# Two-block network on one core: conditioning steps moved from the second feed-forward into the first, and attention values computed token-major

## The chip, the core and the metric

The program runs on one core of a Trainium2 chip. Five engines work side by side, each on its own instructions in program order: PE (TensorE, the matrix engine), DVE (VectorE), ACT (ScalarE), POOL (GpSimd) and SP (SyncE, which here issues nearly all DMA transfers on its queue). They wait for one another by semaphores. The metric is the device time of one execution in microseconds, the median of several runs.

## What is computed

512 tokens of width 1024 go through two blocks in fp32. The first block is feed-forward, mixer, feed-forward. The second is two layers of mixer and mixture of experts, each modulated by vectors made from a condition vector. The two parts that the change touches:

```python
def swiglu(h, w_in, w_out):                      # both feed-forwards of the first block
    g, u = jnp.split(h @ w_in, 2, axis=-1)
    return (jax.nn.silu(g) * u) @ w_out

def adaln(cond, mod_w, mod_b):                   # second block, layer i: mod_w[i] is 1024 x 6144
    m = jax.nn.silu(cond) @ mod_w + mod_b
    return jnp.split(m, 6, axis=-1)
...
sh1, sc1, g1, sh2, sc2, g2 = adaln(c, mod_w[i], mod_b[i])
csh1, csc1, ... = adaln(c_ctx, mod_w[i], mod_b[i])          # layer 0 only, two of six are used
...
def gqa_attend(q, k, v):                         # 8 query heads, 2 key/value heads of width 64
    s = jnp.einsum('bqkgd,bskd->bkgqs', q, k) * (HEAD_DIM ** -0.5)
    p = jax.nn.softmax(s, axis=-1)               # 512 queries against 256 + 512 keys
    return jnp.einsum('bkgqs,bskd->bqkgd', p, v)
...
y = jnp.concatenate([o, multiscale_pool(p, pool_w, pool_scale)], axis=-1) @ w_out
```

## The kernel before

Activations are kept feature-major: a tile has 128 features as partitions and the 512 tokens along the free axis. fp32 products that go through `mm3` (lines 164 to 166) are made from a high and a low part of each operand, three matmuls a step; `hilo` makes the parts, the high one as a cast on ACT (line 159), the low one as a subtraction on DVE (line 160). Weights are loaded by `wload` in tiles of 512 KB into buffers `raw` (line 149, on SP's queue), and `hilo` makes `w` from them.

A feed-forward (`ffn`, line 334) works through the hidden width in four parts of 7, 6, 6 and 3 tiles. In a part, for each tile `gate_up` makes gate and up products (48 matmuls of 512 columns, into a PSUM tile `pb`), `gate` makes the activation tile `act` from them (ACT: silu and cast, DVE: product and low half), and then the down projection runs over eight output tiles, adding to `y` (line 438). The last part is done for one half of the tokens and then the other (h0 and h1, 256 columns); behind each half the boundary normalises: square sums on DVE (line 288), one matmul with ones, a reciprocal square root (lines 261 to 264), the residual (lines 310 and 312) and the input of the next layer (line 299). The mixer that follows starts with h0.

Work that has no place of its own stands in a queue of closures, `bgq`. `ffn` takes `bg` of them behind each tile of `gate_up`, `bg // 3` ahead of each output tile of a down projection, and all that are left ahead of its last part. The modulation vectors are such work: `mv_group` (line 223) queues eight steps for one vector of 1024 entries, each step being one load of 512 KB of `mod_w` into a buffer `aux` (line 231, on SP's queue) and one DVE operation that multiplies it with the silu of the condition (repeated over the partitions, tile `s2`) and sums along the free axis (line 235, 128x1024). For the first two vectors of layer 0 a second such operation does the same with the context's condition (`s3`); its product goes into a buffer `junk` of the pool `k4`, which the tiles `act` come from too. In the kernel before, all 96 steps (112 operations) are queued for the second feed-forward with `bg=5`; the first has `bg=4` and, of the queue, only small preparations of the mixer (`pre_mixer1`).

The attention of the second block (`gqa_head`, line 985) is called for eight heads, four chunks `c` for each of two key/value heads `i`; three streams (the four heads of either `i`, and pooling) are interleaved by `weave`, by written costs. For one head and each of four blocks `n` of 128 queries: the scores go into a PSUM tile `pb` (one of two, 128 queries x 768 keys), DVE takes the maximum (line 998), ACT the exponential with its sum (line 1000) into a buffer `aux` or `raw`, DVE the reciprocal of the sum (line 1001), and DVE or ACT scales the tile by it (lines 1005, 1003). `flip` transposes six blocks on PE (line 1013) and copies them out (lines 1016, 1017). For each two blocks `values` makes six matmuls in plain fp32 (line 1025; each leaves two records in the trace) with the values as weights and 256 query columns moving, into a PSUM tile `pa` of three; ACT copies 64 of its 128 rows to the output tile (line 1026).

The order of the instructions on each engine is set by a scheduler from the order of the code and priorities; it is fixed when the kernel is built.

## Time and profile before

| | us |
|---|---|
| median of 3 runs (1978.03 to 1979.84) | 1978.21 |
| profiled execution, its own time | 1981.37 |
| span of its trace | 1979.5 |
| PE busy | 1829.2 (92%) |
| DVE busy | 1310.9 (66%) |
| ACT busy | 910.8 (46%) |
| mean granted clock of PE | 0.970 of 2.4 GHz |

The stages in that trace, in us from its start: first feed-forward to 402.5, mixer to about 697, second feed-forward to about 1040, mixer of the second block to 1290 (its attention 1135 to 1259), experts to 1550, second layer to the end. With PE busy for 92% of the span, what matters is where it is not, and which other engine or transfer it stands for there. Durations below are those of single instructions; neighbours on an engine overlap by a little, so a stretch of equal ones is best read from start to start.

### The profile page before, as it was taken

To read this page: it belongs to the slowest core of one execution; us is meant where nothing else is said; L and a number is where in the kernel's file an instruction comes from. 1 tells how busy PE (TensorE), PEld (TensorE's weight loads), DVE (VectorE), ACT (ScalarE), POOL (GpSimd) and SP (SyncE) were. 2 spreads that over 40 slices of the span, in tenths; PEclk is the share of its full clock that TensorE was granted. 3 is DMA by queue.
4 is the path that set the end of the run, shared out by engine and by line. 5 is a ranking of instruction groups with operands and counts; after the bars stand their busy time and mean duration, and the time that the engine had idled before them with its cause. 6 is when DMAs were issued, how large, how long until landed. Compare 5 with 4: busy or idle time off the path is not lost. (4 is left out here: it accounts for less than half of the span.)

```text
span 1979.5 us, 25341 instructions
## 1 busy us (share of the span) xinstructions
PE 1829.2 (92%) x9461; PEld 1497.1 (76%) x9461; DVE 1310.9 (66%) x2253; ACT 910.8 (46%) x1463; POOL 163.9 (8%) x133
## 2 busy tenths in 40 slices
PE   4999999999977999989999989979999699979996
PEld 3778888986756888768898867867666688976663
DVE  8877444686775788888448678656654655557773
ACT  5423223465666642222337565526665622345551
POOL 0000000000000000000000000004442000014431
PEclk9999999999998999999999989989999899979998
DMA  8887333232113257888534000538997513559993
GB/s 323 307 311 267 115 93 112 88 120 75 64 32 117 75 191 270 313 315 299 191 106 144 1 0 1 192 131 271 304 319 260 195 60 122 177 202 357 344 353 82
DMA packets 109472, 361.27 MB, mean 183 GB/s; under 512 B 19592, under 2 KB 20256, under 8 KB 109344
## 3 DMA queue, kind: packets, MB, share of 16 engines
q1 hardware_dynamic: 92640, 328.09, 47.0%
q0 software_dynamic: 16128, 29.41, 5.6%
q10 hardware_dynamic: 576, 2.10, 0.3%
q8 instruction: 77, 1.26, 0.3%
q14 instruction: 51, 0.42, 0.1%
HBM read 354.25 MB, written 34.62 MB: 196 GB/s over the span
## 5 line engine op out<-in xcount | busy, mean ns | idle before, releaser
L160 DVE TENSOR_TENSOR w<-raw,w 128x1024 fp32r<-128x1024 f32 (+3 forms) x192 | 221.8, 1160 | 172.5 <-issue 73.1
L159 ACT CAST w<-raw 128x1024 fp32r<-128x1024 f32 (+3 forms) x192 | 191.2, 1000 | 305.4 <-PE pa L166 95.7
L164 PE MATMUL pb<-hh,w 128*128 128x512 f32 (+1 forms) x800 | 288.5, 362 | 19.3 <-ACT hh L159 14.2
L165 PE MATMUL pb<-hl,w 128*128 128x512 f32 (+1 forms) x800 | 289.7, 362 | 4.8 <-DVE hl L160 4.6
L166 PE MATMUL pb<-hh,w 128*128 128x512 f32 (+1 forms) x800 | 289.7, 362 | 2.3 <-DVE w L160 2.3
L164 PEld LDWEIGHTS pb<-hh,w 128*128 128x128 f32 x800 | 151.4, 190 | 45.8 <-ACT hh L159 16.0
L165 PEld LDWEIGHTS pb<-hl,w 128*128 128x128 f32 x800 | 151.7, 190 | 29.7 <-DVE hl L160 7.0
L166 PEld LDWEIGHTS pb<-hh,w 128*128 128x128 f32 x800 | 151.7, 190 | 27.2 <-DVE w L160 4.5
L160 DVE TENSOR_TENSOR k<-raw,k 128x1024 fp32r<-128x1024 f32 x101 | 121.6, 1218 | 65.6 <-ACT k L159 49.1
L164 PE MATMUL pa<-hh,w 128*128 128x512 f32 (+1 forms) x392 | 142.2, 366 | 3.3 <-ACT sq L286 2.0
L1462 PE MATMUL pb<-w,a 128*128 128x512 f32 x304 | 136.9, 593 | 1.9 <-ACT a L1451 1.9
L165 PE MATMUL pa<-hl,w 128*128 128x512 f32 (+1 forms) x392 | 135.5, 347 | 0.0
L166 PE MATMUL pa<-hh,w 128*128 128x512 f32 (+1 forms) x392 | 134.8, 345 | 0.0
L164 PE MATMUL pa<-k,w 128*128 128x512 f32 x304 | 126.3, 415 | 0.0
L235 DVE SCALAR_TENSOR_TENSOR aux<-aux,s 128x1024 f32<-128x1024 f32 x96 | 115.3, 1220 | 16.1 <-DMA aux<-in_mod_w 15.8
L165 PE MATMUL pa<-act,w 128*128 128x512 f32 x304 | 119.1, 392 | 1.8 <-DVE act L160 1.8
L164 PE MATMUL pa<-act,w 128*128 128x512 f32 x304 | 119.1, 392 | 1.6 <-ACT w L159 1.6
L166 PE MATMUL pa<-k,w 128*128 128x512 f32 x304 | 119.8, 394 | 0.0
L166 PE MATMUL pa<-act,w 128*128 128x512 f32 x304 | 119.3, 392 | 0.5 <-DVE w L160 0.5
L165 PE MATMUL pa<-k,w 128*128 128x512 f32 x304 | 119.3, 392 | 0.0
L159 ACT CAST k<-raw 128x1024 fp32r<-128x1024 f32 x101 | 105.2, 1048 | 9.6 <-DMA raw<-in_moe_w 3.3
L1462 PEld LDWEIGHTS pb<-w,a 128*128 128x128 f32 x304 | 57.2, 189 | 60.2 <-issue 53.2
(446 smaller groups left out, 3989.3 us busy)
## 6 DMA issues: line engine op xcount, KB each, us to landing
aux<-in_mod_w SPq DMA_DIRECT2D x96, 512.0 KB
raw<-in_ffn_in SPq DMA_DIRECT2D x88, 512.0 KB
raw<-in_moe_w SPq DMA_DIRECT2D x86, 512.0 KB
aux<-in_w_ada SPq DMA_DIRECT2D x64, 512.0 KB
w<-in_moe_w SPq DMA_DIRECT2D x64, 512.0 KB
k<-in_moe_w SPq DMA_DIRECT2D x42, 512.0 KB
raw<-in_ffn_out SPq DMA_DIRECT2D x32, 384.0 KB
raw<-in_mix_in SPq DMA_DIRECT2D x20, 512.0 KB
```

The costliest lines, as they stand in the source:

```text
L159: self.nc.scalar.copy(hi, src)
L160: return self.nc.vector.tensor_sub(lo, src, hi.bitcast(F32)).ins
L164: mm(p, wh, xh, start=start, stop=False)
L165: mm(p, wh, xl, start=False, stop=False)
L166: mm(p, wl, xh, start=False, stop=stop)
L235: self.nc.vector.scalar_tensor_tensor(junk, w, 1.0, s, op0=OP.mult, op1=OP.mult, accum_out=dst[:, m:m + 1])
L1462: nc.tensor.matmul(py[:, ns], a[:, cs], wt[c][:, ns], start=c == 0, stop=c == 1)
```

## The change

Three vectors of layer 0 (groups 0 to 2 of 12, a quarter) are queued for the first feed-forward, behind `pre_mixer1`: 24 steps with 40 DVE operations, the two silus, and the small sums that end them. The condition tiles come to be known only when their load runs, so `outs` names them and `cvec` holds them. The other 72 steps (72 operations) stay in the second feed-forward, where `s2` is loaded and silu'd again, and `bg` falls from 5 to 3.

In the attention the exponentials are no longer scaled. `values` takes the transposed exponentials as weights (128 keys x 128 queries) and 64 columns of values moving, so that its output has the queries as partitions: for a pair of heads (both `i` of one `c`) eight blocks of 64 columns in one PSUM tile `pt`, the only one of its pool. Behind the pair one reciprocal of the eight columns of sums, one DVE product that scales all 512 columns and moves them to SBUF, four transposes and one ACT copy make the output tile. A pair's values begin when the pair before has both heads done. `flip` now writes one tile `pt` for each block of queries.

```diff
@@ mv_group
                 for i, (s, dst) in enumerate(outs):
+                    s = self.cvec[s] if isinstance(s, str) else s
                     last = i == len(outs) - 1
@@ even mixer
+        pairs = [{"n": 0} for _ in range(4)]
...
-                yield from self.gqa_head(qs[c], i, k, (la, lb)[i], vf, outs[c])
+                pairs[c]["before"] = pairs[c - 1] if c else None
+                yield from self.gqa_head(qs[c], i, k, (la, lb)[i], vf, pairs[c], outs[c])
@@ gqa_head
+        if "l" not in both:
+            both["l"] = self.sm(8, tag="l8", bufs=2)
...
-            nc.scalar.activation(pe[:, :768], sc[:, :768], AF.Exp, bias=mx, accum_out=l)
-            nc.vector.reciprocal(l, l)
-            if (n + 2 * i) % 4 == 0:
-                nc.scalar.activation(pe[:, :768], pe[:, :768], AF.Copy, scale=l)
-            else:
-                nc.vector.tensor_scalar(pe[:, :768], pe[:, :768], l, None, op0=OP.mult)
+            nc.scalar.activation(pe[:, :768], sc[:, :768], AF.Exp, bias=mx, accum_out=both["l"][:, 2 * n + i:2 * n + i + 1])
...
-            t, tx = wt[-1]
+            t = self.k4(F32, "pt")
...
-            a(v3(t, 4)[:, :, js], v3(pt, 4))
-            b(v3(tx, 2)[:, :, js], v3(pc[:, :256], 2))
-        def values(half):
-            t, tx = wt[-1]
-            po = self.psa()[:, :256]
+            a(t[:, :512], pt)
+            b(t[:, 512:768], pc[:, :256])
+            return t
+        def values(n, t):
+            if "po" not in both:
+                assert both["before"] is None or both["before"]["n"] == 2
+                both["po"] = self.pst()
+            o = (2 * n + i) * 64
             for b in range(6):
-                vs = slice(b * P, (b + 1) * P)
-                m = t[:, b * 256:(b + 1) * 256] if b < 4 else tx[:, (b - 4) * 256:(b - 3) * 256]
-                nc.tensor.matmul(po, vf[:, vs], m, start=b == 0, stop=b == 5)
-            nc.scalar.copy(out[r, half * 256:half * 256 + 256], po[r, :])
+                nc.tensor.matmul(both["po"][:, o:o + 64], t[:, b * P:(b + 1) * P], vf[:, b * P + 64 * i:b * P + 64 * i + 64],
+                                 start=b == 0, stop=b == 5)
...
+        l, tk = both["l"], self.pg()
+        nc.vector.reciprocal(l, l)
+        nc.vector.tensor_tensor(tk.rearrange("p (n e) -> p n e", n=8), both["po"].rearrange("p (n e) -> p n e", n=8),
+                                l.unsqueeze(2).to_broadcast((P, 8, 64)), OP.mult)
+        pt = self.psa()
+        for n in range(4):
+            ns = slice(n * P, (n + 1) * P)
+            nc.tensor.transpose(pt[:, ns], tk[:, ns], self.mat("ident"))
+        nc.scalar.copy(out, pt)
@@ main
+        def silus(*which):
+            def go():
+                for n, i in which:
+                    cvec[n] = K.k4(F32, n)
+                    nc.sync.dma_start(cvec[n], A["c_rep"][i])
+                with tc.issue_after(K.gated):
+                    for n, _ in which:
+                        nc.scalar.activation(cvec[n], cvec[n], AF.Silu)
+            return go
...
+        def mod_group(l, g):
+            outs = [("s2", mod[l][g])]
+            if l == 0 and g < 2:
+                outs = [("s3", cmod[g])] + outs
+            K.mv_group(A["mod_w"][l], g, outs)
...
+        K.queue(silus(("s2", 1), ("s3", 2)))
+        for g in range(3):
+            mod_group(0, g)
         K.ffn(h, *ffw("ffn1"), post_boundary(0, to if stop != "ffn1" else None), bg=4, lead=lead)
...
+        K.queue(silus(("s2", 1)))
         for l in range(2):
             for g in range(6):
-                outs = [(s2, mod[l][g])]
...
+                if l or g > 2:
+                    mod_group(l, g)
...
-        K.ffn(to2.h, *ffw("ffn2"), post_boundary(2, to3), bg=5)
+        K.ffn(to2.h, *ffw("ffn2"), post_boundary(2, to3), bg=3)
```

Where the instructions stand, at three places. Names end in numbers that differ between the two kernels, and line numbers are one to a few higher after.

The first place is DVE at the passage from the third to the fourth part of the first feed-forward. `pg_770` and `pg_771` (after: `pg_789`, `pg_790`) are the last sums of the third part's down projection, `w_` the low halves of weights for h0 and h1 (`raw` is the load), and the operations of line 360 (after: 361) make activations of the fourth part. Before:

```order
294 L438 TENSOR_TENSOR pg_771<-pg_771,pa_2389 128x512
295 L160 TENSOR_TENSOR aux_2476<-raw_2474,wk_2475 128x1024
296 L160 TENSOR_TENSOR aux_2482<-raw_2480,wk_2481 128x1024
297 L438 TENSOR_TENSOR pg_771<-pg_771,pa_2415 128x512
298 L160 TENSOR_TENSOR w_2461<-raw_2459,w_2460 128x1024
299 L160 TENSOR_TENSOR aux_2488<-raw_2486,wk_2487 128x1024
300 L360 TENSOR_TENSOR pg_2541<-pg_2541,pb_2492 128x256
301 L160 TENSOR_TENSOR act_2471<-pg_2541,act_2471 128x256
302 L360 TENSOR_TENSOR pg_2595<-pg_2595,pb_2546 128x256
303 L160 TENSOR_TENSOR act_2472<-pg_2595,act_2472 128x256
```

After:

```order
312 L160 TENSOR_TENSOR w_2591<-raw_2589,w_2590 128x1024
313 L236 SCALAR_TENSOR_TENSOR junk_2299,cm_185<-aux_2297,s_370_2047 128x1024
314 L236 SCALAR_TENSOR_TENSOR junk_2304,cm_185<-aux_2302,s_370_2047 128x1024
315 L236 SCALAR_TENSOR_TENSOR aux_2297,mod_169<-aux_2297,s_369_2045 128x1024
316 L236 SCALAR_TENSOR_TENSOR aux_2302,mod_169<-aux_2302,s_369_2045 128x1024
317 L236 SCALAR_TENSOR_TENSOR junk_2309,cm_185<-aux_2307,s_370_2047 128x1024
318 L439 TENSOR_TENSOR pg_790<-pg_790,pa_2506 128x512
319 L236 SCALAR_TENSOR_TENSOR aux_2307,mod_169<-aux_2307,s_369_2045 128x1024
320 L236 SCALAR_TENSOR_TENSOR junk_2314,cm_185<-aux_2312,s_370_2047 128x1024
321 L236 SCALAR_TENSOR_TENSOR junk_2325,cm_185<-aux_2323,s_370_2047 128x1024
322 L361 TENSOR_TENSOR pg_2677<-pg_2677,pb_2628 128x256
323 L236 SCALAR_TENSOR_TENSOR aux_2312,mod_169<-aux_2312,s_369_2045 128x1024
```

Multiply-reduces of five steps now stand between the weights of the fourth part and its first activation; 22 in all stand from here on, ahead of the low half of `act_2609`, the last activation of h0, and `junk_2299` takes the buffer of an activation of the third part (`act_1752`) that the last output tile `pa_2535` still reads.

The second place is SP's queue in the second feed-forward, ahead of the third part's tiles: `raw` are loads of weights, `aux` loads of `mod_w`. Before:

```order
262 L149 DMA raw_6522<-in_ffn_in 128x1024
263 L231 DMA aux_6500<-in_mod_w 128x1024
264 L231 DMA aux_6503<-in_mod_w 128x1024
265 L231 DMA aux_6506<-in_mod_w 128x1024
266 L149 DMA raw_6599<-in_ffn_in 128x1024
267 L231 DMA aux_6509<-in_mod_w 128x1024
268 L231 DMA aux_6512<-in_mod_w 128x1024
269 L231 DMA aux_6582<-in_mod_w 128x1024
270 L149 DMA raw_6605<-in_ffn_in 128x1024
```

After:

```order
272 L149 DMA raw_6474<-in_ffn_in 128x1024
273 L231 DMA aux_6543<-in_mod_w 128x1024
274 L231 DMA aux_6546<-in_mod_w 128x1024
275 L149 DMA raw_6480<-in_ffn_in 128x1024
276 L231 DMA aux_6616<-in_mod_w 128x1024
277 L231 DMA aux_6619<-in_mod_w 128x1024
278 L149 DMA raw_6550<-in_ffn_in 128x1024
279 L231 DMA aux_6622<-in_mod_w 128x1024
280 L231 DMA aux_6692<-in_mod_w 128x1024
```

Three loads of `mod_w` stood between two loads of weights, and two stand there now.

The third place is PE at the end of the attention's last pair, where `out_proj` (lines 164 to 166, with `mix`) follows. Before:

```order
5582 L1025 MATMUL pa_10420<-pt_10376,vf_8903 128x256 [waits DVE_49]
5583 L1025 MATMUL pa_10420<-pt_10376,vf_8903 128x256 x3
5584 L1025 MATMUL pa_10420<-px_1887_10377,vf_8903 128x256 x2
5585 L1025 MATMUL pa_10428<-pt_10388,vf_8903 128x256 [waits DVE_49,Activation_49]
5586 L1025 MATMUL pa_10428<-pt_10388,vf_8903 128x256 x3
5587 L1025 MATMUL pa_10428<-px_1891_10389,vf_8903 128x256 x2
5588 L164 MATMUL pa_10533<-mix_10436,w_10485 128x256
5589 L165 MATMUL pa_10533<-mix_10437,w_10485 128x256
5590 L166 MATMUL pa_10533<-mix_10436,w_10486 128x256
```

After:

```order
5601 L1024 MATMUL pt_10338<-vf_8906,pt_10379 128x64 x6
5602 L1024 MATMUL pt_10338<-vf_8906,pt_10413 128x64 [waits DVE_49]
5603 L1024 MATMUL pt_10338<-vf_8906,pt_10413 128x64 x3
5604 L1024 MATMUL pt_10338<-vf_8906,pt_10413 128x64 [waits Activation_49]
5605 L1024 MATMUL pt_10338<-vf_8906,pt_10413 128x64
5606 L1052 MATMUL pa_10445<-c_89,pg_10442 128x128 [waits DVE_49]
5607 L1052 MATMUL pa_10445<-c_89,pg_10442 128x128 x3
5608 L164 MATMUL pa_10548<-mix_10451,w_10500 128x256 [waits PE_49,Activation_49]
5609 L165 MATMUL pa_10548<-mix_10452,w_10500 128x256
```

The values are twice as many and a quarter as wide, and four transposes (line 1052) that wait for DVE's product `pg_10442` stand between them and `out_proj`.

## Rows read from the trace of the kernel before

**Rows 1.** Windows, whole core: from:to, length, busy us (instructions) by engine, clock, DMA.

```profile
304.10:330.50 26.40, 26.40 (x118) 21.84 (x118) 10.12 (x13) 7.46 (x10) 0.00 (x0) 1.00 0.30 92
349.60:402.53 52.93, 52.66 (x432) 51.90 (x431) 35.36 (x79) 25.82 (x50) 0.00 (x0) 1.00 0.31 99
708.00:759.00 51.00, 51.00 (x226) 42.23 (x226) 50.21 (x86) 12.05 (x16) 0.00 (x0) 1.00 0.67 218
830.00:890.00 60.00, 52.54 (x209) 38.86 (x208) 47.65 (x75) 15.97 (x21) 0.00 (x0) 0.97 0.87 309
1130.00:1260.00 130.00, 115.94 (x603) 95.11 (x602) 97.50 (x191) 82.40 (x165) 0.00 (x0) 0.95 0.10 30
1140.00:1150.00 10.00, 6.27 (x34) 4.46 (x33) 6.80 (x11) 9.05 (x13) 0.00 (x0) 0.95 0.00 1
1150.00:1160.00 10.00, 9.40 (x32) 7.19 (x32) 7.63 (x16) 5.66 (x12) 0.00 (x0) 0.54 0.00 0
```

**Rows 2.** Timeline of DVE, 300 to 403: start us, us, instruction, count.

```profile
305.33 0.96 DVE L160 TENSOR_TENSOR w<-raw,w 128x768 fp32r<-128x768 f32 x1 [4.47 <-issue]
...
318.45 0.69 DVE L160 TENSOR_TENSOR act<-pg,act 128x512 fp32r<-128x512 f32 x1 [0.69 <-ACT act L159]
...
379.82 0.42 DVE L262 SCALAR_TENSOR_TENSOR hf<-pt,hf 128x256 f32<-128x256 f32 x1
...
391.53 2.35 DVE L160 TENSOR_TENSOR w<-raw,w 128x1024 fp32r<-128x1024 f32 x2
...
397.54 0.41 DVE L393 TENSOR_TENSOR pg<-pg,pa 128x256 f32<-128x256 f32 x1
397.87 0.42 DVE L262 SCALAR_TENSOR_TENSOR hf<-pt,hf 128x256 f32<-128x256 f32 x1
```

**Rows 3.** Timeline of PE, first feed-forward's end: first matmuls of four stretches.

```profile
316.18 0.39 PE L164 MATMUL pa<-act,w 128*128 128x512 f32 x1
...
348.82 0.28 PE L164 MATMUL pb<-hh,w 128*128 128x256 f32 x1
...
374.91 0.28 PE L164 MATMUL pb<-hh,w 128*128 128x256 f32 x1
...
402.53 0.38 PE L164 MATMUL pa<-hh,w 128*128 128x256 f32 x1
```

**Rows 4.** Timeline of DVE in the second feed-forward, two conditioning operations.

```profile
712.27 1.22 DVE L235 SCALAR_TENSOR_TENSOR aux<-aux,s 128x1024 f32<-128x1024 f32 x1
...
713.42 1.22 DVE L235 SCALAR_TENSOR_TENSOR aux<-aux,s 128x1024 f32<-128x1024 f32 x1
```

**Rows 5.** Waits, 690 to 1000: engine, line, releaser: us, times, longest.

```profile
PE pb L164 <- ACT w L159: 3.0, 4, 1.1
...
SPq L231 <- DVE aux L235: 147.9, 82, 4.2
SPq L149 <- DVE w L160: 87.4, 26, 30.6
```

**Rows 6.** Lines of DVE, 1130 to 1262: shape, count, busy us, mean ns.

```profile
L1016 DVE COPY pt<-pa 128x512 f32<-128x512 f32 x16 | 10.7, 678 | 0.0
L1005 DVE TENSOR_SCALAR raw<-raw,sm 128x768 f32<-128x768 f32 x12 | 7.4, 614 | 0.1
```

**Rows 7.** Timelines of PE: records of 256, 128 and 20 columns.

```profile
1161.55 1.89 PE L1025 MATMUL pa<-pt,vf 128*128 128x256 f32 x8
1163.27 1.03 PE L1025 MATMUL pa<-px,vf 128*128 128x256 f32 x4
...
500.69 1.05 PE L765 MATMUL pa<-v,wt 128*128 128x128 f32 x8
...
1282.25 1.64 PE L1228 MATMUL pa<-rw,pg 128*128 128x20 f32 x14
1283.73 0.53 PE L1241 MATMUL pb<-c,pg 128*128 128x128 f32 x3
```

**Rows 8.** Waits of PE in the attention, 1130 to 1262.

```profile
PE pb L601 <- ACT aux L1000: 4.9, 6, 1.6
```

More of the change, by code (lines that the diff above doesn't have):

```diff
@@ L983, in even_mixer, with gqa_head @@
         self.out_proj(outs + pools, A["even_out"], evac, done, ahead)
-    def gqa_head(self, q, i, k, kl, vf, out):
+    def gqa_head(self, q, i, k, kl, vf, both, out):
         nc = self.nc
-        r = slice(64 * i, 64 * i + 64)
-        v3 = lambda t, n: t.rearrange("p (c q) -> p c q", c=n)
-        wt = []
+        if "l" not in both:
+            both["l"] = self.sm(8, tag="l8", bufs=2)
         def scores(n):
@@ L1013, in flip @@
                 nc.tensor.transpose(dst, pe[:, b * P:(b + 1) * P], self.mat("ident"))
[L1014 removed]
             a, b = (nc.scalar.copy, nc.vector.tensor_copy)[::-1 if n % 2 else 1]
[L1016 to L1021 removed]
+            a(t[:, :512], pt)
[6 more added lines that the diff above has]
+            o = (2 * n + i) * 64
             for b in range(6):
[L1023 to L1026 removed]
+                nc.tensor.matmul(both["po"][:, o:o + 64], t[:, b * P:(b + 1) * P], vf[:, b * P + 64 * i:b * P + 64 * i + 64],
+                                 start=b == 0, stop=b == 5)
         pe = []
[L1029 removed]
+        last = None
+        for n in range(7):
             if n < 4:
@@ L1032, in gqa_head @@
                 yield 1.0
-            m = n - 2
-            if m < 0:
-                continue
-            if m % 2 == 0:
-                t = self.k4(F32, "pt")
-                wt.append((t, self.k4(F32, "px2")[:, :512]))
-            flip(m, pe[m])
-            yield 0.7
-            if m % 2 == 1:
-                values(m // 2)
-                yield 1.9
+            w = None
+            if 2 <= n < 6:
+                w = flip(n - 2, pe[n - 2])
+                yield 0.7
+            if last is not None:
+                values(n - 3, last)
+                yield 0.9
+            last = w
+        both["n"] += 1
+        if both["n"] < 2:
+            return
+        l, tk = both["l"], self.pg()
[7 more added lines that the diff above has]
+        nc.scalar.copy(out, pt)
+        yield 0.5
     def pool_chunk(self, g, X, pw, edge, out):
@@ L1643, in program, with mod_vecs, ctx_vecs @@
         K.queue(pre_mixer1)
+        cvec = {}
+        def silus(*which):
[7 more added lines that the diff above has]
+            return go
+        mod = [[K.gvec("mod") for _ in range(6)] for _ in range(2)]
+        G2 = [[K.gvec("G2") for _ in range(2)] for _ in range(2)]
+        cmod = [K.gvec("cm") for _ in range(2)]
+        Gc = K.gvec("Gc")
+        def mod_vecs(l, i):
+            for g in range(3 * i, 3 * i + 3):
+                nc.vector.tensor_add(mod[l][g], mod[l][g], K.vec("mod_b", 48 * l + 8 * g, 8))
+            gn = K.vec(("n1g", "n2g")[i], 8 * l, 8)
+            nc.vector.scalar_tensor_tensor(G2[l][i], mod[l][3 * i + 1], 1.0, gn, op0=OP.add, op1=OP.mult)
+        def ctx_vecs():
+            for g in range(2):
+                nc.vector.tensor_add(cmod[g], cmod[g], K.vec("mod_b", 8 * g, 8))
+            nc.vector.scalar_tensor_tensor(Gc, cmod[1], 1.0, K.vec("n1g", 0, 8), op0=OP.add, op1=OP.mult)
+        def mod_group(l, g):
[3 more added lines that the diff above has]
+            K.mv_group(A["mod_w"][l], g, outs)
+            if g == 2 and l == 0:
+                K.queue(ctx_vecs)
+            if g % 3 == 2:
+                K.queue(lambda: mod_vecs(l, g // 3))
+        K.cvec = cvec
+        K.queue(silus(("s2", 1), ("s3", 2)))
+        for g in range(3):
+            mod_group(0, g)
         K.ffn(h, *ffw("ffn1"), post_boundary(0, to if stop != "ffn1" else None), bg=4, lead=lead)
```

32 lines of the change are left out of this document (1 added, 31 removed).

## The prediction, made before the changed kernel was run

> **What bounds the kernel now.** Read the table of windows first, and in it TensorE (PE): where PE is busy for the whole of a window, the stage can't be made faster by relieving another engine. At the end of the first feed-forward (the windows at 304 and 349) PE is full, and VectorE (DVE) has 16.3 us of 26.4 and 17.6 of 52.9 free [rows 1]. In the second feed-forward PE is full beside a full DVE at 708 to 759, and loses 7.5 us between 830 and 890, where the DMA is 87% busy [rows 1]; the waits say that PE stands for casts of weights there, while the DMA queue of SyncE (SP) stands for buffers that DVE has not freed, 148 us for the conditioning's loads and 87 us for the weights' [rows 5]. In the second block's attention PE is idle for 14.1 us of 130, and after ten us with PE busy for 6.3 its granted clock is 0.54 for ten (its lower level, 1.2 GHz, is a half) [rows 1]. The chain of waits that ended last covers the last 8 us only and says nothing of these stages. So there are three terms, and I sum them against the profiled execution: 1981.37 us (span 1979.5), 3.2 above the median of 1978.21.
>
> **Term 1: 24 steps move into the first feed-forward.** Each is a load of 512 KB and one multiply-reduce of DVE over 128x1024, or two (16 of the steps serve two vectors): 40 in all, 1.15 us from start to start [rows 4], 46 us. Two silus on ScalarE (ACT) and three groups of tiny vector operations come along. The DMA has room (30% busy in both windows [rows 1]). On SP's queue up to two conditioning loads come ahead of each weight load of the third part's down projection, ten in a row ahead of the fourth part's last; the mixer's weights stand behind all. DVE has 33.9 us free where 46 must go, and its queue runs in program order, so the question is what stands behind them.
> In the third part, 18 of the 40 stand ahead of the low half of the part's last activation. The silus stand on ACT ahead of the cast whose low half DVE starts at 305.33 [rows 2], so the 18 start at about 304: 18 x 1.15 = 20.6 us, and with six other operations (some 6 us) that activation is ready at about 330.7, against 318.45 + 0.69 = 319.1 before [rows 2]. PE has 45 matmuls of the down projection that don't need it, 0.227 us each (144 from 316.18 to 348.82 [rows 3]), enough until 326.4, and then waits 4.2 us: the third part ends at about 353.
> Then comes the row that decides. `junk_2299`, the next multiply-reduce, writes into the buffer of an activation that PE reads until its last output chunk, so it can't start before PE's third matmul of that chunk's 18: 353 - 15 x 0.23 = 349.5. DVE stands there until PE comes, and 22 start only then. Ahead of the low half of the last activation of the first half of the tokens now stand: 22 x 1.15 = 25.2; four casts of 128x1024 (two in 2.35 [rows 2]) 4.6; two adds of 128x512 (0.68 [rows 6], less the 0.08 by which neighbours overlap) 1.2; eight operations of 128x256 at 0.33 [rows 2] 2.7; small ones 0.5. Sum 34.2: this half's activations are ready at about 384. Its down projection (9 us) ended at 374.91 [rows 3]; now it ends at about 392.5. Casts for the next layer that stand ahead of its last square sums add about 3, so the normalisation that began at 379.82 [rows 2], 4.9 after that end, begins at about 400. From there the mixer's first matmul came 22.7 us later, at 402.53 [rows 2, 3], with five casts between (two are shown [rows 2]) that now lie ahead of it, 5.7: 400 + 17 = 417. PE has the other half's matmuls meanwhile (some of its gate projection is put ahead), but only 53.6 us of work in all after the third part [rows 3], and with three or four us of stalls it stands from about 410. **Term 1: +14.5.** Before, 27.6 us of chain lay beside 27.6 us of the other half's matmuls: the cover was exact, so nothing of the delay is free. Lower bound: 25.2 - 17.6 = 7.6, if DVE never waits again. Upper bound 18, if loads come late as well.
>
> **Term 2: the second feed-forward keeps 72 steps, three a tile where it had five.** SP's order shows three conditioning loads to each weight load in the third part before, two after: a tile of PE's work is 48 matmuls, 10.9 us, and wanted 4 MB, 385 GB/s, where 309 were moved [rows 1]; after, 3 MB, 289 GB/s. That is below what was moved, so the weights should be in time: 7.5 us of idle PE go, and up to 1.8 of the lowered clock (0.97 over 60 us [rows 1]). The experts' constants come later, into a down projection; I find no wait of PE on them and count nothing. **Term 2: -8.5** (-6 if a third stays; -9.3 if all goes).
>
> **Term 3: attention with token-major values.** On DVE 24 scalings of 128x768 (0.61 each [rows 6]) and 32 short reciprocals go; four reciprocals and four products of 128x512 (0.68 for such an operation [rows 6]) come: 14.7 against 2.7. ACT loses eight scalings and twelve copies. On PE 96 matmuls of 256 columns, two records each, become 192 of 64 columns, and 16 transposes come. A record of 256 columns takes 0.215 (eight from 1161.55 to 1163.27 [rows 7]): 192 make 41.3 us. No record of 64 columns is in this trace. Its neighbours are 128 columns (eight in 1.05 with the last one's tail, about 0.10 from start to start) and 20 columns (14 in 1.48, 0.106) [rows 7]: below 128 columns a record gets no shorter. So 384 at 0.10 to 0.106 make 38.4 to 40.7, the transposes 16 x 0.1 = 1.6 more: 40.0 to 42.3, nothing gained or lost.
> The Trainium skill, TensorE: Matmul & The Clock Gate, section LDWEIGHTS, charges a weight load by its 128 columns, about 107 ns, however few columns move; its section Back-to-back issue gap has 81 ns for 128 columns and some 60 cycles for 64 or fewer, by which the values would come to 31 us or to 10 (estimates). The row of 20 columns agrees with the first and decides against the second.
> So PE's work stands, and what can be won is its idle time. 4.9 us of that wait for the exponential that frees a score bank [rows 8], and DVE's and ACT's queues ahead of those get shorter. But the first stall, ahead of 1150, is made of table loads, reductions and exponentials that all stay, less one scaling. New is the end of each pair of heads: PE's four transposes wait for reciprocal, product and two hand-overs. Ahead of them, at three of the four ends, stand the next pair's scores; the last end is bare, about 1 us. **Term 3: -4**: a third of the 14.1 idle, a little clock, less that 1. Ends: -10 (most of the idle and the clock) and +1.
>
> **Sum**: 1981.4 + 14.5 - 8.5 - 4 = 1983.4 for a profiled execution, 1980.2 on the median's scale. About 0.2%, 4 us, is what can be told from no change.
>
> **The rivals.**
> (a) *The moved steps hide.* For: at 708 to 759 PE stayed full beside 40 such operations, DVE at 98% [rows 1]. It holds if `junk_2299` is not held up, or DVE catches up ahead of the half's activations; term 1 is then about +2 and the time 1967.7. Against: the order of DVE's rows, and that the second feed-forward's 40 had no chain of half the tokens behind them.
> (b) *The pair ends are bare.* One PSUM bank holds a pair's values, and the next pair's can't start before the product has read it. Where less than 1 us of scores stands ahead, an end costs PE about 2.3 us (product 0.68, a copy of the same size, four transposes 0.4, reciprocal and hand-overs some 0.6); four cost 9 against the gain of 4: term 3 is +5, and the time 1989.2, slower. For: few matmuls stand there. Against: at three ends they are scores of 1.3 us and more.
> (c) *The second feed-forward isn't relieved*, because the weights' loads wait for their own buffers (87 us [rows 5]) and not behind the others: term 2 is 0, the time 1988.7.
> (d) *Short matmuls go with their columns*: 384 x 0.054 = 20.7 in place of 41.3, and the transposes: 19 less, 1961.2, if PE's work is what then bounds. The 20-column row speaks against it. The Trainium skill's section Back-to-back issue gap (TensorE: Matmul & The Clock Gate) is a rule of this kind.
>
> **How the numbers follow.** Forecast 0.50 (1973 to 1987 of its own): 0.12 faster, 0.26 within 0.2%, 0.12 slower. (a) 0.18: 0.17 faster, 0.01 within. (b) 0.20: 0.17 slower, 0.03 within. (c) 0.08, slower. (d) 0.04, faster. Sums: faster 0.33, same 0.30, slower 0.37. The range, 1966 to 1990, leaves out (d), a third of (a), and of (b) and (c) what lies above, together under 0.2.
>
> **What would show it.** Term 1: PE idle for 7 to 18 us ahead of the mixer's first matmul, which stands at about 417; DVE full from 350 on; a gap of some 4 us near 327. If the mixer starts at 403 to 405, (a) holds. Term 2: PE full from the mixer's end to the end of the feed-forward, and near 290 GB/s in the third part; if not, (c). Term 3: the values' records at 0.10 each, the waits for the exponential about halved, one wait of about 1 us on a pair's product; several of over 2 us mean (b), records at 0.06 mean (d). I am wrong altogether if the stages from 1290 to the end, whose order is nearly the same, move by more than 2 us.

## The result, and the profile after

The changed kernel takes 1997.74 us (median of 4 runs, 1994.47 to 1999.88) against 1978.14 (4 runs, 1978.03 to 1979.84): a ratio of 1.0084, with an interval of 1.0064 to 1.0104. It is 0.84% slower, with the whole interval above 1, and lies above the predicted range. Its profiled execution took 1994.47 us (span 1992.6), the fastest of its four, and that of before 1981.37 us, longer than all four of its timed runs; so the traces differ by 13.1 us where the medians differ by 19.6, and the 6.5 us between can't be put down to a place.

Four anchors on TensorE (PE) divide both traces: the first mixer's first matmul; the matmul behind the 5.2 us wait that ends the first mixer (643.23 after); the first projection of the second block; and the start of the 8.0 us stall ahead of the routing (1329.8 after; the stall ends at 1337.82). The last row goes from there to the end of PE's last matmul, 19.0 us ahead of the end of either trace. From anchor to anchor, in us:

| stage | before | after | difference | predicted |
|---|---|---|---|---|
| up to the mixer's first matmul | 402.5 | 421.7 | +19.1 | +14.5 (term 1) |
| first mixer | 220.1 | 221.5 | +1.4 | 0 |
| second feed-forward | 438.7 | 438.3 | -0.4 | -8.5 (term 2) |
| second block's attention | 255.4 | 248.3 | -7.1 | -4 (term 3) |
| all behind it | 643.8 | 643.7 | 0 | 0 |

Windows of after, columns as in [rows 1]: the first two are the same stretches of time as there, the third is the last 53 us ahead of the mixer, then the second feed-forward's middle, ten us in it, and the attention's 130 us with three tens of it.

```profile
304.10:330.50 26.40, 23.79 (x104) 19.10 (x103) 25.77 (x47) 4.86 (x8) 0.00 (x0) 1.00 0.65 211
349.60:402.53 52.93, 49.63 (x391) 47.99 (x390) 49.00 (x92) 18.57 (x32) 0.00 (x0) 1.00 0.71 233
368.70:421.65 52.95, 42.25 (x319) 39.07 (x317) 47.46 (x105) 24.76 (x49) 0.00 (x0) 0.92 0.50 169
740.00:890.00 150.00, 145.98 (x631) 120.01 (x631) 120.89 (x201) 40.83 (x54) 0.00 (x0) 0.98 0.88 306
780.00:790.00 10.00, 5.98 (x24) 4.44 (x23) 6.80 (x10) 2.04 (x3) 0.00 (x0) 0.91 0.88 316
1150.00:1280.00 130.00, 120.01 (x869) 107.67 (x868) 89.76 (x148) 74.61 (x149) 0.00 (x0) 0.97 0.12 44
1160.00:1170.00 10.00, 7.29 (x40) 5.21 (x39) 6.88 (x10) 9.04 (x14) 0.00 (x0) 1.00 0.00 0
1170.00:1180.00 10.00, 10.00 (x77) 9.18 (x78) 8.34 (x12) 6.69 (x15) 0.00 (x0) 1.00 0.01 2
1220.00:1230.00 10.00, 8.68 (x37) 7.36 (x38) 6.94 (x13) 5.42 (x13) 0.00 (x0) 0.66 0.00 1
```

VectorE (DVE) had 10.1 and 35.4 us busy in the first two windows and now has 25.8 of 26.4 and 49.0 of 52.9: the moved operations are there, and DVE has become the engine that PE waits for. In the 53 us ahead of the mixer PE is idle for 10.7.

### The first feed-forward's end

The timeline of DVE after, 300 to 422, columns as in [rows 2]:

```profile
303.13 1.23 DVE L236 SCALAR_TENSOR_TENSOR junk<-aux,s 128x1024 f32<-128x1024 f32 x1 [2.67 <-ACT s L1665]
...
329.04 0.68 DVE L160 TENSOR_TENSOR act<-pg,act 128x512 fp32r<-128x512 f32 x1
...
348.42 1.22 DVE L160 TENSOR_TENSOR w<-raw,w 128x1024 fp32r<-128x1024 f32 x1 [2.26 <-issue]
349.56 1.22 DVE L236 SCALAR_TENSOR_TENSOR junk<-aux,s 128x1024 f32<-128x1024 f32 x1
...
385.29 0.42 DVE L160 TENSOR_TENSOR act<-pg,act 128x256 fp32r<-128x256 f32 x1 [0.32 <-ACT act L159]
...
400.77 0.42 DVE L263 SCALAR_TENSOR_TENSOR hf<-pt,hf 128x256 f32<-128x256 f32 x1 [1.30 <-ACT hf L262]
...
404.62 1.07 DVE L394 TENSOR_TENSOR pg<-pg,pa 128x256 f32<-128x256 f32 x3
...
418.17 0.42 DVE L263 SCALAR_TENSOR_TENSOR hf<-pt,hf 128x256 f32<-128x256 f32 x1 [0.68 <-ACT hf L262]
```

And PE's beside it; the first row is its first wait in the third part, 352.47 that part's end, 392.85 the end of the down projection of the first half of the tokens, 421.65 the mixer:

```profile
328.53 0.96 PE L164 MATMUL pa<-act,w 128*128 128x512 f32 x3 [2.32 <-ACT act L159]
...
352.47 0.28 PE L164 MATMUL pb<-hh,w 128*128 128x256 f32 x1
...
392.85 0.28 PE L164 MATMUL pb<-hh,w 128*128 128x256 f32 x1
...
414.56 1.22 PE L270 MATMUL pt<-acc,c 128*128 128x256 f32 x2 [3.81 <-DVE acc L289]
418.98 1.22 PE L270 MATMUL pt<-acc,c 128*128 128x256 f32 x2 [3.20 <-DVE acc L289]
421.65 0.58 PE L164 MATMUL pa<-hh,w 128*128 128x256 f32 x1 [1.45 <-ACT hh L159]
```

And ACT's, between PE's second matmul with ones (414.56) and the reciprocal square root made from it:

```profile
413.82 2.53 ACT L287 ACTIVATE sq<-pg 128x256 f32<-128x256 f32 x6
416.37 1.28 ACT L262 ACT_TABLE_LOAD   x1
```

The last activation of the third part is ready at 329.7 where it was at 319.1 [rows 2]; `junk_2299` stands at 349.56 and is the first of the 22 operations, the half's activations are ready at 385.7, and PE's last three waits ahead of the mixer are 8.5 us.

DVE does not stand in front of `junk_2299`: that row has no idle time before it. It stood 2.26 us in front of the row ahead, the low half of a weight at 348.42 (row 312 of the order shown with the change). That is the last of four such waits, 8.1 us together; the last three end at 340.2, 344.3 and 348.4, one output tile of PE apart (18 matmuls of 0.227 us are 4.08), so these operations come one by one as PE finishes an output tile. The profile names no releaser ("issue"); that it is PE is read from this spacing. The third matmul of the last output tile, for which `junk_2299` has to wait, began at 348.84 and was done at 349.2, before DVE came to it.

### The second feed-forward

Waits between 690 and 1000 after (engine, line, releaser: us, times, longest):

```profile
DVE aux L236 <- DMA aux<-in_mod_w: 25.0, 35, 2.2
ACT w L159 <- DMA raw<-in_ffn_out: 9.3, 3, 4.8
PE pa L164 <- ACT act L159: 4.7, 2, 2.6
```

and those of the DMA queue of SyncE (SP), as in [rows 5]:

```profile
SPq L149 <- DVE w L160: 174.3, 46, 30.6
SPq L231 <- DVE aux L236: 59.5, 45, 3.0
```

Waits of ACT and DVE in the same stretch of before:

```profile
ACT w L159 <- DMA raw<-in_ffn_in: 74.1, 19, 6.1
ACT w L159 <- DMA raw<-in_ffn_out: 25.3, 9, 6.8
DVE aux L235 <- DMA aux<-in_mod_w: 15.8, 18, 2.3
```

The weights are no longer late: ScalarE (ACT) waited 99.4 us for them and waits 9.3. But DVE now waits 25.0 us, 35 times, for the conditioning's own loads, and PE stands for activations. One such place, where the first part's down projection needs the part's last activation, in the timeline of all engines of after (start us, us, engine, line, operation, idle time before it; the first row is from the timeline of DVE alone):

```profile
783.27 1.22 DVE L236 SCALAR_TENSOR_TENSOR aux<-aux,s 128x1024 f32<-128x1024 f32 x1 [1.88 <-DMA aux<-in_mod_w]
...
785.42 0.68 DVE L361 TENSOR_TENSOR pg<-pg,pb 128x512 f32<-128x512 f32 x1
...
786.14 0.62 ACT L159 CAST act<-pg 128x512 fp32r<-128x512 f32 x1 [4.06 <-DVE pg L361]
...
786.81 0.51 PE L164 MATMUL pa<-act,w 128*128 128x512 f32 x1 [2.17 <-ACT act L159]
787.27 1.22 DVE L236 SCALAR_TENSOR_TENSOR aux<-aux,s 128x1024 f32<-128x1024 f32 x1 [1.16 <-DMA aux<-in_mod_w]
...
788.42 0.69 DVE L160 TENSOR_TENSOR act<-pg,act 128x512 fp32r<-128x512 f32 x1
...
789.16 0.79 PE L165 MATMUL pa<-act,w 128*128 128x512 f32 x1 [1.84 <-DVE act L160]
```

DVE's order has a multiply-reduce ahead of the product that the last activation of the part is made from, and another between that product and the low half. The first waits 1.88 us for its load and the second 1.16, and PE, whose next matmuls need that activation, waits with them: 2.17 us for the high half and 1.84 for the low one, and 2.57 at the same place in the next part (from 894.7).

### The attention

One timeline row of PE with the values' new matmuls and the one that follows; then waits of PE in the stage:

```profile
1174.71 2.12 PE L1024 MATMUL pt<-vf,pt 128*128 128x64 f32 x18
1176.64 0.48 PE L602 MATMUL pb<-kk,q 128*128 128x512 f32 x1
```

```profile
PE pb L602 <- ACT aux L1003: 4.4, 5, 1.6
PE pa L1052 <- DVE pg L1047: 0.8, 1, 0.8
```

18 records of 64 columns take 1.93 us from start to start, 0.107 each. PE's idle time in 130 us falls from 14.1 [rows 1] to 10.0. The stage begins 20 us later than before; so the ten us at a granted clock of 0.54 (1150 to 1160 [rows 1]) correspond to 1170 to 1180 after, where the clock is 1.00, and one ten at 0.66 has come at 1220.

### The profile page after: what moved, and what is told of

It reads as the page before. It is cut to its first block, busy times and chain, and to the rows that moved or that the text cites. A ratio compares the mean times of both kernels' runs of the same rounds, so it can differ in the third digit from the quotient of the medians.

```text
span 1992.6 us, 25686 instructions
## 1 busy us (share of the span) xinstructions
PE 1833.0 (92%) x9669; PEld 1507.2 (76%) x9669; DVE 1299.9 (65%) x2205; ACT 899.8 (45%) x1444; POOL 163.6 (8%) x133
## 5 line engine op out<-in xcount | busy, mean ns | idle before, releaser
L360 ACT ACTIVATE pg<-pb 128x512 f32<-128x512 f32 (+1 forms) x52 | 27.4, 532 | 166.4 <-PE pb L166 166.4
```

The costliest lines, as they stand in the source:

```text
L360: self.gated = nc.scalar.activation(sv, pg[:, :n], AF.Silu).ins
```

## The experiments

The stages of all kernels, from the same anchors, in us of the profiled execution, with the median and range of the timed runs and the ratio to the kernel before, which had medians of 1980.08, 1980.97 and 1980.98 beside the three groups of runs (the first four kernels, the next four, the last four):

| kernel | mixer starts | first mixer | second feed-forward | attention | time | ratio [interval] |
|---|---|---|---|---|---|---|
| before | 402.5 | 220.1 | 438.7 | 255.4 | 1978.14 | 1 |
| after | 421.7 | 221.5 | 438.3 | 248.3 | 1997.74 | 1.0084 [1.0064, 1.0104] |
| e1 attention only | 403.9 | 220.2 | 434.2 | 246.6 | 1972.63 (1969.3-1976.0) | 0.9965 [0.9953, 0.9978] |
| e2 move only | 426.3 | 220.4 | 439.7 | 254.3 | 2006.39 (2005.0-2009.5) | 1.0134 [1.0116, 1.0153] |
| e3 24 operations for 40 | 408.7 | 218.5 | 429.4 | 248.1 | 1972.14 (1968.3-1975.1) | 0.9959 [0.9944, 0.9975] |
| e4 own buffer for `junk` | 440.9 | 220.3 | 440.3 | 248.1 | 2013.80 (2013.5-2014.3) | 1.0169 [1.0152, 1.0186] |
| e5 group 0 only | 405.5 | 219.9 | 432.9 | 248.1 | 1971.17 (1970.7-1974.6) | 0.9955 [0.9939, 0.9972] |
| e6 16 loads, one operation | 406.9 | 222.8 | 430.1 | 248.2 | 1973.38 (1967.1-1977.0) | 0.9953 [0.994, 0.9967] |
| e7 e3 with five a tile | 406.8 | 220.3 | 435.9 | 249.9 | 1977.19 (1971.7-1980.0) | 0.9976 [0.9962, 0.999] |
| e8 four buffers | 423.1 | 211.6 | 426.9 | 248.4 | 1976.37 (1973.2-1980.0) | 0.9978 [0.9969, 0.9988] |
| e9 ten weight buffers | 428.2 | 216.5 | 441.9 | 249.9 | 1999.41 (1998.0-2001.0) | 1.0089 [1.006, 1.0118] |
| e10 e5, four buffers | 404.4 | 211.7 | 430.7 | 248.1 | 1959.76 (1958.3-1960.2) | 0.9892 [0.9864, 0.992] |
| e11 e1, four buffers | 405.9 | 212.9 | 438.0 | 249.5 | 1967.40 (1961.3-1969.9) | 0.9923 [0.9899, 0.9948] |
| e12 e3, four buffers | 403.9 | 211.6 | 433.3 | 248.1 | 1968.10 (1962.6-1970.8) | 0.9937 [0.9914, 0.996] |

### e1, e2: the two halves of the change apart

e1 is the kernel before with the new `gqa_head` and nothing else; e2 is the kernel after with the old one:

```diff
 # e1, against before
-                yield from self.gqa_head(qs[c], i, k, (la, lb)[i], vf, outs[c])
+                pairs[c]["before"] = pairs[c - 1] if c else None
+                yield from self.gqa_head(qs[c], i, k, (la, lb)[i], vf, pairs[c], outs[c])
...
 # e2, against after
-                pairs[c]["before"] = pairs[c - 1] if c else None
-                yield from self.gqa_head(qs[c], i, k, (la, lb)[i], vf, pairs[c], outs[c])
+                yield from self.gqa_head(qs[c], i, k, (la, lb)[i], vf, outs[c])
```

> The kernel before with the attention of the change alone; conditioning steps as before. If the attention's gain is its own (profiles: 7 us between the start of the attention and the experts' stage), 1971 us, 7 us under the kernel before (5 to 9), and both feed-forwards unchanged. Rival: the gain came only with the other start of the stage, then within 3 us of the kernel before.

> The kernel before with the conditioning steps moved and spread alone; attention as before. If the two parts add up, the kernel after's time plus 7: 1997.7 + 7 = 2004.7 (2001 to 2008), the mixer's first matmul at 421 to 423, and the second feed-forward with stalls at the ends of its first two parts. Rival: the parts work on each other, then 1990 or less.

The attention alone is 0.35% faster, the move alone 1.34% slower, and the stages show each in its own place: -8.8 us of attention in e1 and +23.8 ahead of the mixer in e2. The medians add up (7.5 us gained and 26.3 lost make 18.9 lost, 19.6 measured). So what made the kernel slower is the move alone. The stalls expected of e2 at the ends of the second feed-forward's first two parts are there (5.3 and 1.0 us, and 3.1). Two numbers missed: e2's mixer starts 3.3 us later than the upper end expected, and e1's second feed-forward, whose code is that of before, is 4.5 us shorter in its profiled execution. So differences of some 5 us between two kernels in that stage can't be told from none by one profiled execution each.

### e3, e5, e6: how many operations move

```diff
 # e3, against after: groups 3 to 5 (one operation a load) move, not 0 to 2
-        K.queue(silus(("s2", 1), ("s3", 2)))
-        for g in range(3):
+        K.queue(silus(("s2", 1)))
+        for g in range(3, 6):
...
-                if l or g > 2:
+                if l or g < 3:
 # e5: group 0 alone          e6: groups 3 and 4
+        for g in range(1):
+        for g in range(3, 5):
```

> The kernel after, but the three vectors that move are groups 3 to 5, which have one multiply-reduce a step: 24 loads as before, 24 operations in place of 40; the 16 steps with two operations stay at the start of the second feed-forward. Theory (multiply-reduces in DVE's program order cost the first feed-forward its 19 us): 16 x 1.15 = 18.4 us of DVE less, all of them now ahead of the fourth part, so the mixer's first matmul at 402.5 to 407 and no stall of over 4 us; in the second feed-forward the first part has two operations to a load again and its end no stall; 1966 to 1974 us. Rival (the 24 loads and SP's queue cost it): the mixer still at 418 or later, 1990 or more.

> The kernel after, but only one vector moves into the first feed-forward, group 0 with two operations a step: 8 loads, 16 operations, all of them ahead of the third part's last activation; the other 88 steps stay in the second feed-forward with bg=3. Theory (operations in program order, 1.15 us each): that activation at 304 + 16 x 1.15 + 6 = 328, PE stands about 2 us there, nothing behind, the mixer's first matmul at 404 to 409, where the kernel after has 421.7. Rival (the wait of the thrown-away product for an activation's buffer costs by itself): 412 or later.

> The kernel after, but only groups 3 and 4 move, one operation a step: 16 loads, 16 operations, 12 of them ahead of the third part's last activation. Theory (operations, not loads): 304 + 12 x 1.15 + 6 = 324, ahead of the 326 at which PE needs it, so no stall and the mixer at 402.5 to 405. Rival (loads): twice the loads of group 0, so no earlier than there.

With the same 24 loads and 24 operations for 40 (e3) the mixer starts at 408.7, 13 us sooner than after; with 16 operations, of 8 loads or of 16 (e5, e6), at 405.5 and 406.9. So it is the count of DVE's operations that delays the mixer, not the loads' bytes. (e1, which moves none, starts it at 403.9.) The first wait in e3, PE's timeline:

```profile
323.27 0.50 PE L164 MATMUL pa<-act,w 128*128 128x512 f32 x1 [1.68 <-ACT act L159]
324.38 0.79 PE L165 MATMUL pa<-act,w 128*128 128x512 f32 x1 [0.60 <-DVE act L160]
```

No stall of over 4 us was expected, and there is none. The mixer came 1.7 us later than the upper end expected for e3, and 1.9 later for e6. In e6 no stall was expected at all, but PE stood 1.6 and 0.8 us near 321, and the granted clock was 0.91 from 320 to 340, in e3 as well. In e5 it stood 0.4 and 0.5 us where 2 were expected.

### e4: is it the wait of `junk_2299`?

```diff
-    def __init__(self, tc, A, ctx, nk4=25, nhf=5, nraw=4, nw=11, nmv=3):
+    def __init__(self, tc, A, ctx, nk4=24, nhf=5, nraw=4, nw=11, nmv=3):
...
+        self.junk = self.cst(1024)
...
-                    junk = w if last else self.k4(F32, "junk")
+                    junk = w if last else self.junk
```

> The kernel after, but the product that is thrown away goes to a tile of its own (pool k4 one smaller), so no multiply-reduce waits for PE to free an activation. The order puts 32 of the 40 ahead of the third part's last activation: 304 + 32 x 1.15 + 6 = 347. Theory (the number of operations in program order, whatever they wait for): PE stands about 21 us near 326, the mixer's first matmul at 420 to 426, time 1995 to 2003. Rival (the wait of that one buffer is the cause): DVE done early, the mixer at 410 or earlier, 1987 or less.

Nothing holds `junk` up any more, and the kernel is the slowest of all. PE's timeline in the third part:

```profile
347.66 1.22 PE L164 MATMUL pa<-act,w 128*128 128x512 f32 x2 [19.45 <-ACT act L159]
```

With the buffer's wait gone, the operations stand ahead of the part's last activation and PE waits 19.45 us at once (21 expected). The mixer starts at 440.9, 15 us beyond the upper end expected, and the time lies 11 us beyond its own: in the order that resulted, all gate matmuls of the second half (393.65 to 411.09) stand ahead of three quarters of the first half's down projection (54 of its 72 matmuls, 411.5 to 418.7). This kernel has one activation buffer less and another order at the end, so its 441 is no clean price; but the 19.45 us lie ahead of that, and they are enough for the rival to fall: where DVE's work shows depends on the order, and the price is that of DVE's operations ahead of an activation, whatever holds them.

### e7: five steps a tile again

```diff
 # against e3
-        K.ffn(to2.h, *ffw("ffn2"), post_boundary(2, to3), bg=3)
+        K.ffn(to2.h, *ffw("ffn2"), post_boundary(2, to3), bg=5)
```

> The run e3 (one-output vectors moved) with bg=5 in the second feed-forward in place of 3. If bg thins the loads of the conditioning there, the weights come late again in the second and third part and the time is 5 to 10 us over e3: 1977 to 1982. Rival (the rate is set by DMA and buffers and bg only by when the steps end): within 3 us of e3, 1969 to 1975.

The second feed-forward takes 6.5 us more than in e3, and ACT waits for weights again (in e3 these rows are 5.2 and 2.1). Waits in e7:

```profile
ACT w L159 <- DMA raw<-in_ffn_in: 33.6, 11, 6.9
ACT w L159 <- DMA raw<-in_ffn_out: 21.6, 6, 6.3
```

So the thinner spread does what term 2 said where nothing else takes its place: 6.5 us in this stage, 3.4 by the ratios, whose intervals overlap. That ACT waits for the weights again is the firmer sign.

### e8, e9: the buffers of the conditioning's loads

```diff
 # e8, against after
-    def __init__(self, tc, A, ctx, nk4=25, nhf=5, nraw=4, nw=11, nmv=3):
+    def __init__(self, tc, A, ctx, nk4=25, nhf=5, nraw=4, nw=10, nmv=4):
 # e9
+    def __init__(self, tc, A, ctx, nk4=25, nhf=5, nraw=4, nw=10, nmv=3):
```

> The kernel after with four buffers for conditioning loads in place of three (and one fewer for the low halves of weights). Theory (in the second feed-forward the multiply-reduces that stand ahead of a part's last activation wait for their loads, and three buffers let too few loads run ahead): DVE's waits for these loads fall from 25 us to under 12, the stalls at two part ends from 6.6 to under 3, time 1988 to 1993. Rival (the DMA is the limit there, 86 to 96% busy): waits and time as in the kernel after, 1995 to 2000.

> The changed kernel with ten weight buffers in place of eleven, three buffers for the conditioning's loads as it has. It tells apart which half of the edit of the kernel with four buffers gave the 21 us. Theory (the fourth buffer gave the second feed-forward's gain): the stalls of 2.2, 1.8 and 2.6 us at the ends of its parts stay, it takes 658 to 661 us from the mixer's first matmul to the second block's first projection, and the time is 1994 to 2002. Rival (another order of the work, which follows from ten buffers, gave it: the first mixer alone was some 10 us shorter there): 640 to 650, and the time 1978 to 1988.

A fourth buffer has to be paid with a weight buffer, so e9 pays without buying. Waits of DVE and PE between 690 and 1000, first e8:

```profile
DVE aux L236 <- DMA aux<-in_mod_w: 17.4, 19, 2.4
PE pa L164 <- DVE pg L439: 0.5, 1, 0.5
```

DVE's timeline of e8 at the place shown for after (785 there), where the product stands at 773.38:

```profile
773.98 1.22 DVE L236 SCALAR_TENSOR_TENSOR aux<-aux,s 128x1024 f32<-128x1024 f32 x1
...
775.12 0.69 DVE L160 TENSOR_TENSOR act<-pg,act 128x512 fp32r<-128x512 f32 x1
```

and the waits of e9:

```profile
DVE aux L236 <- DMA aux<-in_mod_w: 32.3, 32, 2.7
PE pa L164 <- ACT act L159: 10.4, 2, 5.9
```

With four buffers no wait of PE for an activation is left and the second feed-forward takes 426.9 us; with three it takes 441.9 (after: 438.3), with stalls of 4.5 and 5.9 us at the two ends of parts. In e8 a multiply-reduce still stands between the product and the low half, and it does not wait. The DMA is as busy in both from 740 to 890 (0.88; 315 GB/s in e8, 299 in e9), so the rival, by which the DMA is the limit, falls. SP's queue stands 26.2 us for a conditioning buffer in e8 and 65.3 in e9. So three buffers were what kept the conditioning's loads late. One number missed: DVE's waits for these loads fell from 25.0 to 17.4 us and not to under 12; what is left of them is no longer ahead of an activation that PE needs. e8 gained 12 us more than the lower end expected, most of it in a stage that the theory left out: its first mixer takes 211.6 us for 221.5. About half of that goes with ten weight buffers (216.5 in e9).

### e10, e11, e12: four buffers with less moved

e10, e11 and e12 are e5, e1 and e3 with the line of e8:

```diff
+    def __init__(self, tc, A, ctx, nk4=25, nhf=5, nraw=4, nw=10, nmv=4):
```

> Only the first group of conditioning moves (8 loads, 16 operations), with four buffers for the conditioning's loads and ten for the weights. Theory (the two gains add, since one lies at the end of the first feed-forward and one in the second): the mixer's first matmul at 404 to 408, then 640 to 646 us to the second block's first projection (652.8 with three buffers), in all 1957 to 1965, better than the kernel with the attention alone (1972.6). Rival (the stage was 638 us only because 24 steps and not 8 had moved): 650 to 654, and 1969 to 1973.

> The kernel before with the attention's change alone and four buffers for the conditioning's loads, ten for the weights: no step moves. Theory (five loads a tile ask for more than the DMA moves, whatever the buffers): the loads for the weights still come late in the second feed-forward, ScalarE's casts wait for some 60 to 90 us, the stage takes 649 to 655 us (654.4 with three buffers), the time is 1967 to 1973. Rival (a fourth buffer alone removes the stalls): 640 to 645 us, 1958 to 1963.

> 24 steps of one operation each move (groups 3 to 5), four buffers for the conditioning's loads and ten for the weights. Theory: the mixer's first matmul at 405 to 410, then 637 to 643 us to the second block's first projection (647.9 with three buffers, 638.5 with four where the moved steps had 40 operations), in all 1960 to 1967. Rival (with three buffers this stage had no stall of TensorE over 1.2 us in the feed-forward, so a fourth finds nothing to win): 646 to 649, and 1970 to 1974.

e10, at 1959.76 us, beats both kernels, before by 1.1% (interval 0.8 to 1.4%) and after by 1.9%, as its theory expected in each number. But the place is not the one that was meant: against e5 the second feed-forward gains 2.2 us and the first mixer 8.2. In e11 and e12 too all of the gain is in the mixer (7.3 and 6.9), and the second feed-forward is 3.8 and 3.9 us longer than with three buffers, which is within the scatter seen in e1; PE's idle time there grew by 2 us in both, and the mean granted clock fell from 0.995 to 0.981 and from 0.991 to 0.983. There was no long stall at the ends of parts to remove in e3, as e12's rival said; e12's 644.9 us for the two stages lie between its two ranges, and its time is 1.1 us over the upper end of its theory's. The theory of e11 fell although its times came: ACT waits 12.7 us for weights, not 60 to 90, and PE stands for them near 758, 762 and 784 (3.0, 3.7 and 1.7 us) and not behind 850 as in e1. Waits in e11:

```profile
ACT w L159 <- DMA raw<-in_ffn_out: 9.3, 5, 4.9
ACT w L159 <- DMA raw<-in_ffn_in: 3.4, 1, 3.4
```

The mixer's share is open in its cause. The buffers of the conditioning's loads also hold the first mixer's exponentials (`aux`), and three of its waits shrink from e5 to e10: the cast of a weight (3.5 us to none), the exponentials' tile ahead of the next scores (4.9 to 3.2) and `xc` (3.9 to 1.1). But the order of the work differs too, and e9 has half of the gain without the fourth buffer.

## Why the prediction was wrong

**Term 1 had the cause right and was 4.6 us short**, 1.1 beyond its upper end of 18. Predicted and measured, along the chain: the first added operation at 304, 303.13; the third part's last activation at 330.7, 329.7; PE's wait there 4.2, 2.3; the part's end 353, 352.5; `junk_2299` at 349.5, 349.56; the half's activations at 384, 385.7; its down projection's end at 392.5, 392.85; the normalisation at 400, 400.77; PE standing from 410, 410.75.

One of these agreements is luck. "DVE stands there until PE comes" is not what the trace shows: DVE stood for the weight's low half in front of `junk_2299`, and that operation's own wait was over when DVE reached it. Both waits follow PE's output tiles and end within 1 us of each other (348.4 and 349.2), and the operation between them takes 1.15 us; so the one that the prediction named cost nothing. In this order the 22 operations would stand where they do without it.

The last step of the sum failed: "400 + 17 = 417". From normalisation to mixer it took 20.9 us. I had taken five casts (5.7 us) out of the 22.7 of before, because they now lay ahead, and had put nothing in their place. First, only four lie in that stretch of before: the two shown [rows 2] and these, 4.6 us by 1.15 each:

```profile
390.00 1.22 DVE L160 TENSOR_TENSOR w<-raw,w 128x1024 fp32r<-128x1024 f32 x1
...
396.40 1.22 DVE L160 TENSOR_TENSOR w<-raw,w 128x1024 fp32r<-128x1024 f32 x1
```

Second, the other half's work had been held up too and now stands in this half's way. Eight adds of its down projection (line 394, from 404.62, 0.34 us each) stand among this half's residual operations, where before they came behind them. Six of its squares stand on ACT ahead of the table load and the reciprocal square root, for which DVE is idle for 0.68 us at 418.17. How the 3.9 us divide among these is not shown.

That DVE's operations in program order are the cause of the whole is shown by e2, e3, e5 and e6. That it hangs on the one wait of `junk_2299`, as my case for rival (a) had it, is refuted by e4. Rival (a) falls.

**Term 2 was the step that failed**: -8.5 became -0.4, +1.0 with the first mixer. (The mixer's 1.4 us show no sign of the loads: PE is idle there for 22.9 us where it was 24.9, and the mean granted clock is 0.94 for 0.96. Its first 20 us run at 0.88, for 1.00 before, behind the stalls of term 1; that these 1.4 us therefore belong to term 1 is argued, not tested.) "The weights should be in time" was right: ACT's waits for them fell from 99.4 to 9.3 us. "So 7.5 us of idle PE go" was not. I asked whether the weights' loads would come in time and not whether the conditioning's own would, though DVE's queue holds their operations ahead of the part's last activations, and though [rows 1] had shown at 708 to 759 what kept that harmless: 16 of the steps there had two operations each, so DVE and not the DMA set the pace (67% busy). These are the steps that moved away. After, one load feeds one operation, and in the second part, where PE had stood before, the loads came no thinner: the DMA moves 312 GB/s from 822 to 897, for 306 from 801 to 873 before (289 predicted). They were only through sooner; in the third part it moves 83 GB/s (928 to 994), where it moved 260 (909 to 975). SP's queue stands 59.5 us for one of the three conditioning buffers and 174.3 us for the weights', with conditioning loads behind them in its order, and DVE stands for the loads. e3 shows what the two-operation steps did: it moves as many loads but leaves these 16 in place, and the stage takes 429.4 us: 9.3 less than before, 4.8 less than e1 and 8.9 less than after, near what term 2 had promised. e8 and e9 show the buffers (426.9 against 441.9), e7 that the spread counts where the loads are in time. (The rates of 385 and 289 were counted from six and four conditioning loads a tile, where `bg` queues five and three.) Rival (c) named the right result, 0, by a wrong mechanism: the weights were relieved.

**Term 3**: -4 predicted, -7.1 measured (-8.8 in e1), within the ends given. Over the stage PE's idle time fell by 3.2 us (17.3 to 14.1) and its mean granted clock rose from 0.97 to 0.99 (1.00 in e1); the rest of the gain goes with the clock. The values' records take 0.107 us, as the row of 20 columns had said, so rival (d) falls; one product is waited for, 0.8 us, so rival (b) falls. Two details differ: the waits for the exponential did not halve (4.9 [rows 8] to 4.4), and the ten us at a clock of 0.54 went, which I had counted as "a little clock"; how much the clock gives back differs between executions of the same attention (8.8 us of gain in e1).

**The sum.** +14.5 - 8.5 - 4 = +2 was predicted and +19.1 + 1.0 - 7.1 = +13.1 measured; of the 11 us between, 9.5 are term 2's (with the first mixer), 4.6 term 1's, and term 3 gave 3.1 back. The stages behind 1290 moved by 0.1 us, as they should. The range, 1966 to 1990, was too narrow by construction: the two terms that could fail together, the mixer later than 417 and the second feed-forward not relieved, stood as separate cases, and their sum, 1981.4 + 18 - 4 = 1995.4 in a profiled execution with my own upper bound for term 1, was in none. It is within 1 us of the profile of after, in part by luck: term 1 went beyond that bound, and term 3 gave more.

## What to carry to other kernels

Work moved into an engine's free time costs nothing only if nothing that the bottleneck waits for stands behind it in that engine's program order: count the operations ahead of each such result, here 18 and 22, and move so few that they fit (e5: 16 operations cost 3 us, 1.6 beside e1, which moves none; 40 cost 19). When a stream of loads is thinned, ask which of its consumers stands in order ahead of something urgent, and whether its buffers let the loads run ahead; the relief of one queue can end in a wait for the other. Terms whose failures can coincide belong into one case of the range.

## What the runs showed of the hardware

- The granted clock falls behind idle time of PE that a change makes itself. In after PE was idle for most of 410.75 to 421.65, and its clock was 0.82 from 400 to 420 and 0.84 from 420 to 440. In the attention the ten us at 0.54 followed ten with PE busy for 6.3 [rows 1]; after the change PE is busy for 7.3 in the same ten (1160 to 1170) and the next ten are at 1.00.
- A matmul record of 64 columns took 0.107 us, no less than one of 128 (about 0.10) or of 20 (0.106) [rows 7].
- Executions of one kernel spread more than I had assumed from three runs: the 9 runs of before beside e9 to e12 go from 1976.5 to 1986.9, and the mean granted clock of e11's five from 0.965 to 0.972, the fastest run with the highest.
